# Softmax factors inside the turning matrix, the compressed rows as one block, and the scan's sample rows for all channel blocks at once

## The chip, the cores and the metric

The kernel runs on one core of one Trainium2 chip. The metric is device time in microseconds, the median of several executions. Engines are named as in the profile: PE (TensorE matmul), PEld (its weight load), DVE (VectorE), ACT (ScalarE), POOL (GpSimd) and SP (SyncE, which here only issues DMAs).

## What is computed

One inference step of two trunk layers over 520 rows: a prompt of 512 positions and 8 sample rows of one position each, model width 1024. Layer 0 is a Mamba-2 scan (2048 channels in 16 blocks of 128) beside an attention branch of 16 heads of 64, joined by one output projection; layer 1 is a convolution module; behind each stands a ConvFFN. The parts that the change touches, shortened:

```python
# attention, per query row t and head h: two softmaxes that are used here
p_c = masked_softmax(s_c, m_c)         # over 31 compressed rows
p_s = masked_softmax(s_s, m_s)         # selected rows (for the prompt: all earlier rows)
p_w = masked_softmax(s_w, m_w)         # window rows
o = g[..., 0:1] * (p_c @ vc) + g[..., 1:2] * (p_s @ vs) + g[..., 2:3] * (p_w @ vw)

# scan, a sample row: one step of the recurrence from a stored state
h_t = exp(dt * a) * h_0 + dt * outer(x, B);  y = C @ h_t + d_skip * x
y = rms_norm((y * silu(z)) per group)
out = concat([y_ssm, y_nsa]) @ w_out
```

All tensors are fp32, and the products of the large weights are kept to fp32 quality by splitting.

## The kernel before

**Split products.** A weight or an activation is split into hi + lo (`split`, L292 to L294: ACT copies to hi, DVE subtracts to lo), and a product is three matmuls (`mm3`, L312 to L314). `wload` (L296) stages a weight block of 128x1024 in a buffer of the pool `raw` (three buffers, open for the whole kernel), from where `split` writes it to a second pool.

**Attention.** `attention(hg)` runs for four groups of four heads, each over four blocks `b` of 128 query rows: 16 steps. A step forms scores of 128x`nw` for `nw = 128*(b+1)` keys, selected (`r=0`) and window (`r=1`) apart, and exponentials `pt` (`Ps`). It multiplies each `pt` by gate over sum (`mx[:, 2]`), 8 scalings a step, some on ACT (L1178), the others on DVE (L1180). Then `turned` (L1182) turns four blocks of 128x128 by PE transposes against the identity into `pT`, splits it into `pth` and `ptl`, and two matmuls of 512 columns add V times these to `po` (L1199, L1200). A step has 2(b+1) such parts and one last part for the compressed rows `pc`, where `pT` has 32 partitions. Between the steps, up to 32 blocks of another projection, `xz_tile` (48 matmuls each), and steps of the sample rows' attention are issued; they fill PE while softmax work goes on elsewhere. The last three steps have little of this left.

**Scan.** `scan_group(g, beside)` runs for four groups of four channel blocks t. Each of the 16 steps loads rows `xs` and `cum`, builds decays and does chunk products; seven small DVE operations (L1387 to L1395) of 8 columns serve its sample rows. `beside` issues blocks of the output projection (kg=0) between. After the scan `begin` (L1652) opens the residual `h` and the pools of the next layers, and the kg=1 third of the output projection follows from `wout` (L1283). `state_rows` finishes the sample states on DVE, two pieces a step.

**What sets the order.** A scheduler with a simulated timeline orders the instructions of each engine and frees pool buffers by dependence; pool sizes and the side on which a pool lies decide which loads can be issued early.

Of the kernel before, what the change touches and what calls it, by code (L numbers as in the profile page):

```python
# [40 lines left out]
ACT_NORM = (0, 2)  # L41
# [217 lines left out]
def step_kernel(ctx: ExitStack, tc: tile.TileContext, I, O):  # L259
# [4 lines left out]
    P["raw"] = ctx.enter_context(tc.tile_pool(name="raw", bufs=3, side="right"))  # L264
# [12 lines left out]
    def VV(name):  # L277
        o, n = VEC[name]
        return vec[:, o:o + n]
# [404 lines left out]
    def mixer(begin):  # L684
# [43 lines left out]
        VC = ap.tile([32, 2, 2, 64], F32R, name="VC")  # L728
# [23 lines left out]
        b2v = tp.tile([64, 128], F32, name="b2v", bufs=1)  # L752
# [5 lines left out]
        def behind_x(hf, ins):  # L758

            with tc.issue_after(ins):  # L760
# [6 lines left out]
                nc.scalar.dma_start(b2v, I["b2v"].to_broadcast([64, 128]))  # L767
# [112 lines left out]
        for kv in range(2):  # L880
# [44 lines left out]
        def compress(b):  # L925
# [4 lines left out]
            for kv in range(2):  # L930
# [20 lines left out]
                else:  # L951
                    for g in range(2):
                        nc.tensor.matmul(ps[0:64, g * 64:g * 64 + 64], hid[:, g], w2[:, 128:192], start=True, stop=True)
                    nc.vector.scalar_tensor_tensor(vcS[:, b], ps[0:64], 0.5, b2v, op0=ALU.mult, op1=ALU.add)
# [39 lines left out]
        def xz_tile(g, t):  # L994
# [20 lines left out]
            nc.sync.dma_start(spill[g * 10 + t], th)  # L1015

# [85 lines left out]
        def attention(hg, rows_of):  # L1102
            g = hg // 2
            qh = tp.tile([128, 2, S], F32, tag="qh", name="qh", bufs=1)
            nc.sync.dma_start(qh, d_q[hg])
            for b in range(4):
                step = 4 * hg + b
                nw = 128 * (b + 1)
                QS = tp.tile([128, 4, 128], F32R, tag="QS", name="QS")
                for par in range(2):  # L1110
                    sl, ot = slice(par * 64, par * 64 + 64), slice(64 - par * 64, 128 - par * 64)
                    src = qh[sl, :, b * 128:b * 128 + 128]
# [20 lines left out]
                pc = tp.tile([128, 4, 32], F32, tag="pc", name="pc", bufs=2)  # L1133
# [40 lines left out]
                for hh in range(4):  # L1174
                    for r in range(2):
                        p = Ps[hh][:, r, 0:nw]
                        if r == 0 and b in ACT_NORM:
                            nc.scalar.activation(p, p, AF.Copy, scale=mx[:, 2, hh, r:r + 1])  # L1178
                        else:
                            nc.vector.tensor_scalar(p, p, mx[:, 2, hh, r:r + 1], None, op0=ALU.mult)  # L1180

                def turned(ps4, kn):  # L1182

                    pT = gen(512, "pT")
                    for hh in range(4):
# [116 lines left out]
        def scan_group(g, beside):  # L1302
# [21 lines left out]
            if g >= HG:  # L1324
                later = state_rows(tp, g)
# [372 lines left out]
```

## Time and profile before

| what | value |
|---|---|
| runs shown | 1958.25, 1958.77 and 1962.19 us, median 1958.77 |
| profiled execution | 1961.67 us, of which its span is 1959.9 |
| PE busy | 94% of the span, clock 0.97 on average |
| DVE, ACT, POOL busy | 72%, 50%, 10% |
| attention, 280 to 668 us; scan, 668 to 860 us | 388 and 192 us |

The table's first line is the time of executions with no profile beside it; the profiled one is 2.9 us above their median. A matmul row's duration includes its way through the pipeline, so the distance from one start to the next says more of PE's demand than the duration does. The stretches are cut where the profile's rows change: from 280 to 610 the attention's steps have projection blocks between them, from 610 to 668 they have nearly none, and 856.8 to 874.2 is the border between the scan and the rest.

### The profile page before, as it was taken

What the parts mean: (1) busy time and instruction counts of PE and PEld (TensorE: products, weight loads), DVE (VectorE), ACT (ScalarE), POOL (GpSimd) and SP (SyncE); (2) the same over time, 40 slices, a digit from 0 to 9 for tenths busy, and PEclk for the clock granted to TensorE, in tenths of its full rate; (3) what the DMA queues carried; (4) which work ended last, traced back from release to release, by engine and by line L of the source; (5) the groups of instructions that cost most, each with busy time, mean ns of one, the idle gap of its engine ahead of it and who ended that gap; (6) DMA issues with size and microseconds to landing.
All of it is one profiled execution on the core that took longest, in us unless ns stands there. A gap on an engine that the chain in (4) does not pass through costs nothing.

```text
span 1959.9 us, 38005 instructions
## 1 busy us (share of the span) xinstructions
PE 1835.2 (94%) x14449; PEld 1706.1 (87%) x14449; DVE 1415.3 (72%) x3385; ACT 974.4 (50%) x2093; POOL 189.5 (10%) x226
## 2 busy tenths in 40 slices
PE   6998889999998799998999999999989899999997
PEld 5997888988887588987999999998667789999997
DVE  5764768888887698968667766574786865666766
ACT  3223446676666577646555433355127755444433
POOL 0000021101000003130000211001111000000000
PEclk9999998999998799989999999999999999999999
DMA  8446254444321274543245433222433223444421
GB/s 296 114 140 197 76 190 130 149 138 129 126 90 57 92 243 136 157 143 100 87 143 165 132 105 109 87 81 53 119 107 119 87 87 116 122 119 120 148 62 49
DMA packets 125947, 240.90 MB, mean 123 GB/s; under 512 B 16499, under 2 KB 63236, under 8 KB 125444
## 3 DMA queue, kind: packets, MB, share of 16 engines
q1 hardware_dynamic: 120676, 221.45, 36.9%
q0 software_dynamic: 4000, 13.73, 2.2%
q10 hardware_dynamic: 1088, 3.29, 0.5%
q8 instruction: 114, 1.87, 0.4%
q14 instruction: 69, 0.57, 0.1%
HBM read 200.75 MB, written 30.88 MB: 118 GB/s over the span
## 4 chain that ended last, share of the span: by engine, by line
PE 43%; DVE 5%; ACT 3%; DMA 2%; issue 1%; SPq 0%; POOL 0%; DVEq 0%; ACTq 0%; POOLq 0%
PE up L312 8%; PE up L313 8%; PE up L314 8%; PE dn L312 4%; PE dn L313 4%; PE dn L314 4%; PE dn L624 2%; PE pw L312 1%; PE pw L313 1%; PE pw L314 1%; PE ns L333 1%; DMA raw_dn<-in_w_down 1%; DVE xf L385 1%; DVE h L387 1%; DVE facc L631 1%
## 5 line engine op out<-in xcount | busy, mean ns | idle before, releaser
L312 PE MATMUL dn<-gh,wh_dn 128*128 128x256 f32 (+1 forms) x704 | 198.0, 285 | 4.8 <-ACT gh L463 2.6
L314 PE MATMUL dn<-gh,wl_dn 128*128 128x256 f32 (+1 forms) x704 | 198.9, 284 | 0.0
L313 PE MATMUL dn<-gl,wh_dn 128*128 128x256 f32 (+1 forms) x704 | 198.4, 283 | 0.0
L451 DVE SCALAR_TENSOR_TENSOR c<-up,vec,c 128x511 f32<-128x511 f32 (+2 forms) x216 | 138.9, 645 | 16.1 <-ACT c L448 15.7
L312 PEld LDWEIGHTS dn<-gh,wh_dn 128*128 128x128 f32 x704 | 131.5, 189 | 6.8 <-DVE facc L478 3.7
L313 PEld LDWEIGHTS dn<-gl,wh_dn 128*128 128x128 f32 x704 | 133.1, 189 | 0.1
L314 PEld LDWEIGHTS dn<-gh,wl_dn 128*128 128x128 f32 x704 | 132.8, 189 | 0.0
L464 POOL TENSOR_TENSOR gl<-gm,gh 128x520 fp32r<-128x520 f32 (+2 forms) x54 | 61.8, 1145 | 700.6 <-ACT gh L463 700.5
L446 DVE TENSOR_TENSOR up<-up,rsx 128x520 f32<-128x520 f32 (+2 forms) x108 | 65.0, 603 | 81.5 <-PE up L314 79.9
L478 DVE TENSOR_TENSOR facc<-dn,facc 128x256 f32<-128x256 f32 (+1 forms) x160 | 66.2, 423 | 66.4 <-PE dn L314 66.1
L293 ACT ACTIVATE wh_up<-raw_up 128x1024 fp32r<-128x1024 f32 x68 | 72.0, 1058 | 71.8 <-PE up L313 46.5
L312 PE MATMUL acc<-x0hm,wh_xz 128*128 128x256 f32 x320 | 96.3, 301 | 6.9 <-ACT u L1001 4.5
L294 DVE TENSOR_TENSOR wl_up<-raw_up,wh_up 128x1024 fp32r<-128x1024 f32 x68 | 83.1, 1222 | 23.0 <-ACT wh_up L293 22.9
L314 PE MATMUL acc<-x0hm,wl_xz 128*128 128x256 f32 x320 | 94.3, 295 | 0.0
L313 PE MATMUL acc<-x0lm,wh_xz 128*128 128x256 f32 x320 | 94.1, 294 | 0.0
L313 PE MATMUL acc<-x1lm,wh_xz 128*128 128x264 f32 x320 | 92.8, 290 | 0.0
L312 PE MATMUL acc<-x1hm,wh_xz 128*128 128x264 f32 x320 | 92.6, 289 | 0.0
L448 ACT ACTIVATE c<-up,vec 128x520 f32<-128x520 f32 (+2 forms) x108 | 74.9, 695 | 34.8 <-DVE up L446 34.4
L314 PE MATMUL acc<-x1hm,wl_xz 128*128 128x264 f32 x320 | 92.1, 288 | 0.0
L293 ACT ACTIVATE wh_dn<-raw_dn 128x1024 fp32r<-128x1024 f32 (+1 forms) x48 | 47.4, 988 | 87.7 <-PE dn L313 62.8
L294 DVE TENSOR_TENSOR ptl<-pT,pth 128x512 fp32r<-128x512 f32 (+1 forms) x96 | 65.0, 684 | 25.8 <-ACT pth L293 25.6
L293 ACT ACTIVATE pth<-pT 128x512 fp32r<-128x512 f32 (+1 forms) x96 | 56.3, 595 | 53.1 <-PE pT L1186 49.9
(584 smaller groups left out, 6859.7 us busy)
## 6 DMA issues: line engine op xcount, KB each, us to landing
raw_up<-in_w_up SPq DMA_DIRECT2D x68, 512.0 KB, 3.8
raw_xz<-in_w_in SPq DMA_DIRECT2D x40, 512.0 KB, 4.8
raw_dn<-in_w_down SPq DMA_DIRECT2D x32, 512.0 KB, 3.7
raw_wo<-in_w_out SPq DMA_DIRECT2D x24, 512.0 KB, 4.2
raw_pw<-in_w_pw SPq DMA_DIRECT2D x24, 512.0 KB, 3.8
spill<-uth SPq DMA_DIRECT2D x40, 260.0 KB, 2.0
st<-in_st SPq DMA_DIRECT2D x40, 256.0 KB, 4.2
cc<-in_c_cmp SPq DMA_DIRECT2D x64, 128.0 KB, 2.6
```

The source lines that it names most:

```text
L293: nc.scalar.activation(hi, src, AF.Copy)
L294: (eng or nc.vector).tensor_sub(lo, src, hi.bitcast(F32))
L312: nc.tensor.matmul(ps, hi[:, wc], xh, start=first, stop=False)
L313: nc.tensor.matmul(ps, hi[:, wc], xl, start=False, stop=False)
L314: nc.tensor.matmul(ps, lo[:, wc], xh, start=False, stop=last)
L333: nc.tensor.matmul(ps, ones, acc[:, :n], start=i < group, stop=i == len(ks) - 1)
L446: nc.vector.tensor_mul(u(a, e0), u(a, e0), rv[:, a:e0])
L448: nc.scalar.activation(c[:, rs], u(r0, r1), AF.Identity, bias=V("fb", l * 44 + mt), scale=W(2, mt))
L451: nc.vector.scalar_tensor_tensor(c[:, a:e], u(a - d, e - d), W(2 - d, mt), c[:, a:e], op0=ALU.mult, op1=ALU.add)
L464: nc.gpsimd.tensor_sub(gl[:, rs], gm[:, rs], gh[:, rs].bitcast(F32))
L478: nc.vector.tensor_add(f, ps, f)
L624: nc.tensor.matmul(ps[i * 32:i * 32 + 32], cw[m][:, 4 * q + i], x4[m][:, i, cs], start=q == 0, stop=q == NQ[m] - 1)
```

## The change

Four edits and what they need of memory. (1) The factors `mx[:, 2]` are no longer applied to `pt`: one DVE product makes a tile `dg` of eight diagonal blocks (identity times factor), and each 128x128 block of `pt` is turned by an ordinary fp32 matmul against its diagonal block. (2) The compressed rows of four heads are turned as one 128x128 block, with `VC` padded to a block diagonal, and stand first in `po`. (3) `qh` is loaded per step. (4) The sample rows of the scan: their first part is computed once for all 16 channel blocks (`sample_rows`), the rest once a group (`sample_group`), `cum` of these rows comes by two DMAs of their own, and `state_rows` for the last group start with group 2. The pool `raw` becomes two: `rawm` with two buffers until the scan's end, and a new `raw` with three that `begin` opens.

```diff
-    P["raw"] = ctx.enter_context(tc.tile_pool(name="raw", bufs=3, side="right"))
...
-        VC = ap.tile([32, 2, 2, 64], F32R, name="VC")
+        VC = ap.tile([128, 2, 4, 2, 64], F32R, name="VC")
...
+                hid4 = tp.tile([128, 2, 4, 32], F32, tag="cc4", name="chid4", bufs=1)
+                nc.vector.tensor_copy(hid4, hid[:, :, None, :].to_broadcast([128, 2, 4, 32]))
-                    nc.tensor.matmul(ps[0:32, g * 64:g * 64 + 64], hid[:, g], w2[:, 128:192], start=True, stop=True)
-                vc = tp.tile([32, 2, 64], F32, tag="ub", name="vcP", bufs=2)
-                nc.vector.scalar_tensor_tensor(vc.rearrange("p g d -> p (g d)"), ps[0:32], 0.5, b2v[0:32], op0=ALU.mult,
-                                               op1=ALU.add)
-                split(VC[:, :, 0], VC[:, :, 1], vc)
+                    nc.tensor.matmul(ps[:, g * 64:g * 64 + 64], hid4[:, g].rearrange("p h c -> p (h c)"), w2[:, 128:192],
+                                     start=True, stop=True)
+                vc = tp.tile([128, 2, 64], F32, tag="ub", name="vcP", bufs=2)
+                nc.vector.scalar_tensor_tensor(vc.rearrange("p g d -> p (g d)"), ps, 0.5, b2v, op0=ALU.mult, op1=ALU.add)
+                nc.vector.memset(VC.bitcast(F32), 0.0)
+                for hh in range(4):
+                    rw = slice(32 * hh, 32 * hh + 32)
+                    split(VC[rw, :, hh, 0], VC[rw, :, hh, 1], vc[rw])
...
+            if t < 4:
+                nc.gpsimd.tensor_copy(smp[:, m, 0], th[:, S:T])
...
-            qh = tp.tile([128, 2, S], F32, tag="qh", name="qh", bufs=1)
-            nc.sync.dma_start(qh, d_q[hg])
+                qh = tp.tile([128, 2, 128], F32, tag="qh", name="qh", bufs=2)
+                nc.sync.dma_start(qh, d_q[hg][:, :, b * 128:b * 128 + 128])
-                    src = qh[sl, :, b * 128:b * 128 + 128]
+                    src = qh[sl]
...
-                pc = tp.tile([128, 4, 32], F32, tag="pc", name="pc", bufs=2)
+                pc = tp.tile([128, 4, 32], F32, tag="pc", name="pc", bufs=1)
...
+
+                dg = tp.tile([128, 4, 2, 128], F32, tag="dg", name="dg", bufs=1)
+                nc.vector.tensor_mul(dg.rearrange("p h r q -> p (h r) q"), ident[:, None, :].to_broadcast([128, 8, 128]),
+                                     mx[:, 2].rearrange("p h r -> p (h r)")[:, :, None].to_broadcast([128, 8, 128]))
+
+                def parted(pT):
+                    ph, pl = (tp.tile([128, 512], F32R, tag="pt" + p, name="pt" + p, bufs=THB)[:, :pT.shape[-1]]
+                              for p in "hl")
+                    split(ph, pl, pT)
+                    return ph, pl
+
+
+                po = gen(512, "po")
+
+                pT = gen(128, "pT")
+                nc.tensor.transpose(pT, pc.rearrange("p h k -> p (h k)"), ident)
+                ph, pl = parted(pT)
+                    for p in (ph, pl):
+                        nc.tensor.matmul(po[:, hh * 128:hh * 128 + 128], VC[:, g, hh].rearrange("p a d -> p (a d)"), p,
+                                         start=hh == 0 and p is ph, stop=False)
+                for n in range(b + 1):
-                        p = Ps[hh][:, r, 0:nw]
-                        if r == 0 and b in ACT_NORM:
-                            nc.scalar.activation(p, p, AF.Copy, scale=mx[:, 2, hh, r:r + 1])
-                        else:
-                            nc.vector.tensor_scalar(p, p, mx[:, 2, hh, r:r + 1], None, op0=ALU.mult)
-
-                def turned(ps4, kn):
-
-                    pT = gen(512, "pT")
-                    for hh in range(4):
-                        nc.tensor.transpose(pT[0:kn, hh * 128:hh * 128 + 128], ps4[hh], ident)
-                    ph, pl = (tp.tile([128, 512], F32R, tag="pt" + p, name="pt" + p, bufs=THB)[0:kn] for p in "hl")
-                    split(ph, pl, pT[0:kn])
-                    return ph, pl
-
-
-                po = gen(512, "po")
-                parts = [(VB[:, 1 - r, n, g], [p[:, r, n * 128:n * 128 + 128] for p in Ps], 128)
-                         for n in range(b + 1) for r in range(2)]
-                parts.append((VC[:, g], [pc[:, hh] for hh in range(4)], 32))
-                for k, (v, ps4, kn) in enumerate(parts):
-                    ph, pl = turned(ps4, kn)
-                    v = v.rearrange("p a d -> p (a d)")
-                    nc.tensor.matmul(po, v, ph, start=k == 0, stop=False)
-                    last = nc.tensor.matmul(po, v, pl, start=False, stop=k == len(parts) - 1)
+                        pT = gen(512, "pT")
+                        for hh in range(4):
+                            nc.tensor.matmul(pT[:, hh * 128:hh * 128 + 128], Ps[hh][:, r, n * 128:n * 128 + 128],
+                                             dg[:, hh, r], start=True, stop=True)
+                        ph, pl = parted(pT)
+                        v = VB[:, 1 - r, n, g].rearrange("p a d -> p (a d)")
+                        nc.tensor.matmul(po, v, ph, start=False, stop=False)
+                        last = nc.tensor.matmul(po, v, pl, start=False, stop=n == b and r == 1)
...
-            cum = pool.tile([128, 2, 528], F32, tag="cum", name="cum", bufs=1 if g == t == 0 else XSB)
+            cum = pool.tile([128, 2, S], F32, tag="cum", name="cum", bufs=1 if g == t == 0 else XSB)
-            q.dma_start(cum, d_rows[k:k + 2, :].rearrange("(o h) t -> o h t", o=1).to_broadcast([128, 2, 528]))
+            q.dma_start(cum, d_rows[k:k + 2, 0:S].rearrange("(o h) t -> o h t", o=1).to_broadcast([128, 2, S]))
...
+
+
+        cd = tp.tile([128, 16, 2 * NB], F32, name="cumS")
+        for r in range(2):
+            nc.gpsimd.dma_start(cd[r * 64:r * 64 + 64], d_rows[r::2, S:528].rearrange("(o m) t -> o m t", o=1)
+                                .to_broadcast([64, 16, 2 * NB]))
+        xsk = tp.tile([128, 16, NB], F32, name="xskS")
+
+        def sample_rows():
+
+            nc.scalar.activation(smp[:, :, 1], cd[:, :, 0:NB], AF.Exp)
+            nc.vector.tensor_mul(xsk, smp[:, :, 0], VV("dsk")[:, :, None].to_broadcast([128, 16, NB]))
+            nc.vector.tensor_mul(smp[:, :, 0], smp[:, :, 0], cd[:, :, NB:])
+
+        def sample_group(g, y, bcs):
+
+            gs = slice(4 * g, 4 * g + 4)
+            ys = tp.tile([128, 4, NB], F32, tag="ys", name="ys", bufs=2)
+            nc.vector.tensor_mul(hC[:, gs], hC[:, gs], smp[:, gs, 1])
+            nc.vector.tensor_mul(ys, smp[:, gs, 0], bcs[:, 1][:, None, :].to_broadcast([128, 4, NB]))
+            nc.vector.tensor_add(hC[:, gs], hC[:, gs], xsk[:, gs])
+            nc.vector.tensor_add(y[:, :, S:T], hC[:, gs], ys)
...
-            if g >= HG:
-                later = state_rows(tp, g)
+            if g == HG - 1:
+                later = state_rows(tp, HG)
+            if g == 0:
+                sample_rows()
-                E = tp.tile([128, T], F32, tag="E", name="E", bufs=EB)
+                E = tp.tile([128, S], F32, tag="E", name="E", bufs=EB)
-                    nc.scalar.activation(E[sl, 128:T], cum[sl, r, 128:T], AF.Exp)
+                    nc.scalar.activation(E[sl, 128:S], cum[sl, r, 128:S], AF.Exp)
...
-
-                dtx, es = smp[:, 4 * g + t, 0], E[:, S:T]
-                nc.vector.tensor_copy(smp[:, 4 * g + t, 1], es)
-                ys = tp.tile([128, 2, NB], F32, tag="ys", name="ys", bufs=2)
-                for r in range(2):
-                    sl = slice(r * 64, r * 64 + 64)
-                    nc.vector.tensor_mul(dtx[sl], xs[sl, S:T], cum[sl, r, T:528])
-                nc.vector.tensor_mul(ys[:, 0], hC[:, 4 * g + t], es)
-                nc.vector.tensor_mul(ys[:, 1], dtx, bcs[:, 1])
-                nc.vector.tensor_add(ys[:, 0], ys[:, 0], ys[:, 1])
-                nc.vector.scalar_tensor_tensor(y[:, t, S:T], xs[:, S:T], V("dsk", 4 * g + t), ys[:, 0],
-                                               op0=ALU.mult, op1=ALU.add)
+                if t == 0:
+                    sample_group(g, y, bcs)
...
+        P["raw"] = ctx.enter_context(tc.tile_pool(name="raw", bufs=3))
-    with tc.tile_pool(name="wum", bufs=3, side="right") as P["wu"]:
+    with tc.tile_pool(name="rawm", bufs=2, side="right") as P["raw"], \
+            tc.tile_pool(name="wum", bufs=3, side="right") as P["wu"]:```

The last attention step on PE. Names: `pT` is the turned block, `pth` and `ptl` its halves, `VB` and `VC` the values, `cst` the identity, `dg` the diagonal blocks. Before:

```order
L1186 MATMUL pT<-cst_77,pt 128x128 x4
L1199 MATMUL po<-pth,VB 128x512
L1200 MATMUL po<-ptl,VB 128x512
L1186 MATMUL pT<-cst_77,pc 32x128 x4
L1199 MATMUL po<-pth,VB 128x512
L1200 MATMUL po<-ptl,VB 128x512
L1639 MATMUL oT<-cst_77,osS 128x128
L1199 MATMUL po<-pth,VC 128x512
L1200 MATMUL po<-ptl,VC 128x512
```

The same step after the change:

```order
L1198 MATMUL po<-pth,VC 128x128
L1198 MATMUL po<-ptl,VC 128x128
L1204 MATMUL pT<-dg,pt 128x128 x8
L1208 MATMUL po<-pth,VB 128x512
L1209 MATMUL po<-ptl,VB 128x512
L1204 MATMUL pT<-dg,pt 128x128 x4
L1208 MATMUL po<-pth,VB 128x512
L1209 MATMUL po<-ptl,VB 128x512
```

The compressed part has moved from the end of the step to its beginning, and each turn is now a matmul against `dg`.

The border after the scan on SP, the DMA issues up to the first weights of the next layers. Names: `raw_wo` stages w_out, `raw_us` the next layer's w_up, `hst`, `Bb`, `st` belong to states. Before:

```order
L302 DMA raw_wo<-in_w_out 128x1024
L1331 DMA zt<-spill_151 128x520
L1358 DMA o_sp<-hst 128x128
L302 DMA raw_wo<-in_w_out 128x1024
L1358 DMA o_sp<-hst 128x128
L1467 DMA Bb<-d_bc 128x4x128
L1472 DMA st<-in_st 128x512
L302 DMA raw_wo<-in_w_out 128x1024
L1472 DMA st<-in_st 128x512
L1658 DMA h<-in_x 128x8x256
L1658 DMA h<-in_x 128x8x264
L302 DMA raw_wo<-in_w_out 128x1024 x3
```

The same border after the change:

```order
L1391 DMA o_sp<-hst 128x128
L1364 DMA zt<-spill_151 128x520
L1391 DMA o_sp<-hst 128x128 x3
L1490 DMA Bb<-d_bc 128x4x128
L1495 DMA st<-in_st 128x512 x2
L1681 DMA h<-in_x 128x8x256
L1681 DMA h<-in_x 128x8x264
L300 DMA raw_wo<-in_w_out 128x1024 x8
L300 DMA raw_us<-in_w_up 128x1024 x6
```

All eight loads of the kg=1 weights now stand behind the load of `h`; before, five of them stood ahead of it (three are in these rows, two in earlier ones).

## Rows read from the trace of the kernel before

**Rows 1.** The page: busy time of each engine, and the chain of waits by engine

```profile
PE 1835.2 (94%) x14449; PEld 1706.1 (87%) x14449; DVE 1415.3 (72%) x3385; ACT 974.4 (50%) x2093; POOL 189.5 (10%) x226
...
PE 43%; DVE 5%; ACT 3%; DMA 2%; issue 1%; SPq 0%; POOL 0%; DVEq 0%; ACTq 0%; POOLq 0%
```

**Rows 2.** Four stretches: length, busy us (instructions) of each engine, clock, DMA share, GB/s

```profile
280.00:610.00 330.00, 317.51 (x2460) 288.36 (x2460) 279.65 (x921) 213.50 (x537) 29.22 (x44) 0.97 0.41 128
340.00:360.00 20.00, 20.00 (x174) 18.24 (x174) 18.59 (x49) 14.12 (x32) 1.59 (x3) 1.00 0.39 115
610.00:668.00 58.00, 47.98 (x190) 31.78 (x191) 41.21 (x116) 31.28 (x78) 0.00 (x0) 0.76 0.07 21
668.00:860.00 192.00, 176.13 (x1409) 160.62 (x1409) 171.24 (x501) 132.66 (x338) 41.44 (x44) 0.95 0.54 170
```

**Rows 3.** Groups on PE, 280 to 610 | busy us, mean ns

```profile
L1186 PE MATMUL pT<-cst,pt 128*128 128x128 f32 x248 | 40.9, 273 | 0.0
L1186 PE MATMUL pT<-cst,pc 128*32 128x128 f32 x52 | 7.8, 272 | 0.0
```

**Rows 4.** Timeline of PE, four turns: start, us from first to last end

```profile
582.02 0.60 PE L1186 MATMUL pT<-cst,pt 128*128 128x128 f32 x4
```

**Rows 5.** Timeline of PE, four matmuls of F32 operands in the scan

```profile
723.90 1.06 PE L1349 MATMUL states<-xde,BT 128*128 128x128 f32 x8
724.79 0.60 PE L1341 MATMUL xT<-cst,xs 128*128 128x128 f32 x4
```

**Rows 6.** Timeline of PE, a product of the compressed rows

```profile
568.77 0.49 PE L1199 MATMUL po<-pth,VC 32*128 32x512 f32 x1
569.19 0.38 PE L313 MATMUL acc<-x0lm,wh_xz 128*128 128x256 f32 x1
```

**Rows 7.** Groups on DVE, 280 to 670 | busy us, mean ns | idle before

```profile
L1180 DVE TENSOR_SCALAR pt<-pt,mx 128x256 f32<-128x256 f32 (+3 forms) x96 | 31.1, 389 | 0.2
L294 DVE TENSOR_TENSOR wl_xz<-raw_xz,wh_xz 128x1024 fp32r<-128x1024 f32 x29 | 35.3, 1218 | 5.3 <-ACT wh_xz L293 5.3
L294 DVE TENSOR_TENSOR ptl<-pT,pth 128x512 fp32r<-128x512 f32 (+1 forms) x96 | 65.0, 684 | 25.8 <-ACT pth L293 25.6
L1141 DVE TENSOR_TENSOR pc<-pc,mc 128x128 f32<-128x128 f32 x16 | 4.5, 283 | 0.1
```

**Rows 8.** Groups on ACT, the same stretch

```profile
L1178 ACT ACTIVATE pt<-pt,mx 128x128 f32<-128x128 f32 (+1 forms) x32 | 13.6, 503 | 1.3 <-DVE mx L1173 1.3
L293 ACT ACTIVATE pth<-pT 128x512 fp32r<-128x512 f32 (+1 forms) x96 | 56.3, 595 | 53.1 <-PE pT L1186 49.9 <-DVE ptl L294 2.2 <-DVE mx L1128 0.5
```

**Rows 9.** Waits, 280 to 670: who, for whom; us in total, times, longest

```profile
ACT wh_xz L293 <- PE acc L313: 11.6, 11, 2.7
```

**Rows 10.** Timeline, last attention step

```profile
648.19 0.20 DVE L1172 RECIPROCAL mx<-mx 128x8 f32<-128x8 f32 x1 [0.31 <-ACT pt L1169]
652.99 0.60 ACT L293 ACTIVATE pth<-pT 128x512 fp32r<-128x512 f32 x1 [3.94 <-PE pT L1186]
```

**Rows 11.** Timeline at the border after the scan

```profile
856.80 0.58 PE L312 MATMUL acc<-x0hs,wh_wo 128*128 128x256 f32 x1 [0.22 <-ACT x0hs L293]
863.39 1.35 SPq L1658 DMA_DIRECT2D h<-in_x  x2
863.39 2.96 ACT L293 ACTIVATE wh_wo<-raw_wo 128x1024 fp32r<-128x1024 f32 x3 [1.51 <-POOL x1ls L294]
865.74 3.43 SPq L302 DMA_DIRECT2D raw_wo<-in_w_out  x3
```

**Rows 12.** Busy time by stretch, the border

```profile
856.80:874.20 17.40, 16.63 (x105) 15.31 (x106) 9.93 (x14) 6.42 (x13) 6.47 (x8) 0.80 0.54 191
```

**Rows 13.** Chain of waits at the border: start, us, what

```profile
865.74 8.29 DMA raw_wo<-in_w_out
```

**Rows 14.** Groups on DVE in the scan, two of the six removed

```profile
L1391 DVE TENSOR_TENSOR smp<-xs,cum 64x8 f32<-64x8 f32 x30 | 5.5, 184 | 4.7 <-DMA cum<-d_rows 2.6 <-DMA xs<-spill 1.8
L1392 DVE TENSOR_TENSOR ys<-hC,E 128x8 f32<-128x8 f32 x16 | 2.5, 157 | 0.0
```

More of the change, by code (lines that the diff above doesn't have):

```diff
@@ L40 @@
 HOLD = 6
-ACT_NORM = (0, 2)
 NQ = (5, 4, 4, 4, 4, 6, 7, 7)
@@ L751, in mixer @@
         w2 = tp.tile([128, 192], F32, name="w2", bufs=1)
-        b2v = tp.tile([64, 128], F32, name="b2v", bufs=1)
+        b2v = tp.tile([128, 128], F32, name="b2v", bufs=1)
         pe = tp.tile([128, 2, 2, 8], F32, name="pe", bufs=1)
@@ L766, in behind_x @@
                 nc.scalar.dma_start(alr, I["alr"].to_broadcast([128, 32]))
-                nc.scalar.dma_start(b2v, I["b2v"].to_broadcast([64, 128]))
+                nc.scalar.dma_start(b2v, I["b2v"].to_broadcast([128, 128]))
                 nc.scalar.dma_start(pe.rearrange("p a b c -> p (a b c)"), I["pe"])
@@ L953, in compress @@
                         nc.tensor.matmul(ps[0:64, g * 64:g * 64 + 64], hid[:, g], w2[:, 128:192], start=True, stop=True)
-                    nc.vector.scalar_tensor_tensor(vcS[:, b], ps[0:64], 0.5, b2v, op0=ALU.mult, op1=ALU.add)
+                    nc.vector.scalar_tensor_tensor(vcS[:, b], ps[0:64], 0.5, b2v[0:64], op0=ALU.mult, op1=ALU.add)
         prep, scores_of, softmaxes = nsa_sample(mp, gen, C, tp, knew, qs, kcS, PT, pnT, gS, gather)
@@ L1173, in attention @@
                 nc.vector.tensor_mul(mx[:, 2], mx[:, 2], gTsw[:, b, 4 * hg:4 * hg + 4])
-                for hh in range(4):
-                    for r in range(2):
-                        p = Ps[hh][:, r, 0:nw]
-                        if r == 0 and b in ACT_NORM:
-                            nc.scalar.activation(p, p, AF.Copy, scale=mx[:, 2, hh, r:r + 1])
-                        else:
-                            nc.vector.tensor_scalar(p, p, mx[:, 2, hh, r:r + 1], None, op0=ALU.mult)
-                def turned(ps4, kn):
-                    pT = gen(512, "pT")
-                    for hh in range(4):
-                        nc.tensor.transpose(pT[0:kn, hh * 128:hh * 128 + 128], ps4[hh], ident)
-                    ph, pl = (tp.tile([128, 512], F32R, tag="pt" + p, name="pt" + p, bufs=THB)[0:kn] for p in "hl")
-                    split(ph, pl, pT[0:kn])
+                dg = tp.tile([128, 4, 2, 128], F32, tag="dg", name="dg", bufs=1)
@@ new lines, in attention @@
+                nc.tensor.transpose(pT, pc.rearrange("p h k -> p (h k)"), ident)
[7 more added lines that the diff above has]
+                        pT = gen(512, "pT")
+                        for hh in range(4):
+                            nc.tensor.matmul(pT[:, hh * 128:hh * 128 + 128], Ps[hh][:, r, n * 128:n * 128 + 128],
[4 more added lines that the diff above has]
+                        last = nc.tensor.matmul(po, v, pl, start=False, stop=n == b and r == 1)
@@ L1300, in nsa_out @@
             return part
+        cd = tp.tile([128, 16, 2 * NB], F32, name="cumS")
+        for r in range(2):
+            nc.gpsimd.dma_start(cd[r * 64:r * 64 + 64], d_rows[r::2, S:528].rearrange("(o m) t -> o m t", o=1)
[12 more added lines that the diff above has]
+            nc.vector.tensor_add(y[:, :, S:T], hC[:, gs], ys)
         def scan_group(g, beside):
@@ L1385, in scan_group @@
                     next(later, None)
-                dtx, es = smp[:, 4 * g + t, 0], E[:, S:T]
-                nc.vector.tensor_copy(smp[:, 4 * g + t, 1], es)
-                ys = tp.tile([128, 2, NB], F32, tag="ys", name="ys", bufs=2)
-                for r in range(2):
-                    sl = slice(r * 64, r * 64 + 64)
-                    nc.vector.tensor_mul(dtx[sl], xs[sl, S:T], cum[sl, r, T:528])
-                nc.vector.tensor_mul(ys[:, 0], hC[:, 4 * g + t], es)
-                nc.vector.tensor_mul(ys[:, 1], dtx, bcs[:, 1])
-                nc.vector.tensor_add(ys[:, 0], ys[:, 0], ys[:, 1])
-                nc.vector.scalar_tensor_tensor(y[:, t, S:T], xs[:, S:T], V("dsk", 4 * g + t), ys[:, 0],
-                                               op0=ALU.mult, op1=ALU.add)
+                if t == 0:
+                    sample_group(g, y, bcs)
                 nc.vector.tensor_mul(y[:, t], y[:, t], zt)
@@ L1664, in begin @@
         return after
-    with tc.tile_pool(name="wum", bufs=3, side="right") as P["wu"]:
+    with tc.tile_pool(name="rawm", bufs=2, side="right") as P["raw"], \
+            tc.tile_pool(name="wum", bufs=3, side="right") as P["wu"]:
         new = mixer(begin)()
```

## The prediction, made before the result was known

> **What bounds the kernel now.** I read the page first: PE is busy for 94% of the span, DVE for 72%, and the chain that ended last goes through PE for 43% and through DVE for 5% [rows 1]. PE is therefore the engine to count on, but an average over the whole span says nothing of the parts that change, so the second view is the busy time by stretch [rows 2]. The attention with projection blocks between its steps (280 to 610 us) has PE busy for 317.5 of 330 us and DVE for 279.7; its last steps (610 to 668) have PE for 48.0 of 58 at a granted clock of 0.76; the scan (668 to 860) has PE for 176.1 and DVE for 171.2 of 192.
>
> Busy time overstates PE, because the rows of pipelined matmuls overlap. Its real demand I take from a stretch in which it never rests: 340 to 360, with 174 matmuls in 20.0 us at full clock [rows 2], which is 0.115 us each. The 2460 matmuls of 280 to 610 then ask for 283 us, 86% of the stretch, which leaves 47 us of slack in pieces; the 1409 of the scan ask for 162 of 192. PE is nearly the bound in the attention, and DVE (85% busy there) is close behind. The third view is the list of waits and groups: ACT's conversion `pth` stands idle for 49.9 us because PE has not yet turned `pT` [rows 8]. The engine that is waited for in the attention is PE, and its turns are what is waited for.
>
> **The turns.** A transpose on PE is one record; four of them last 0.60 us, with 0.27 for one, so they follow each other every (0.60-0.27)/3 = 0.11 us [rows 3, 4]. An ordinary matmul of two fp32 operands with 128 columns is seen in the scan: four matmuls have eight records, and the next work starts 0.89 us after the first [rows 5], 0.22 each. The change makes all 320 turns of `pt` (16 steps, 20 blocks on average) into such matmuls, so each costs 0.11 more: 35.8 us of PE in all, 27.8 for the 248 that stand before 610 [rows 3] and 8.1 for the 72 behind.
>
> That this is the wrong direction is also a rule: the Trainium skill's page "Perfetto Trace Analysis", section "Transposes", says to make a logical transpose by the transpose instruction and not by a standard matmul, since it skips the arithmetic. The trace agrees, with 0.11 against 0.22 us.
>
> **The compressed rows.** Turning them as one block takes three of four turns away, 39 of 52 before 610 [rows 3]: -4.3 us. Their product has 32 partitions and 512 columns and takes 0.42 us [rows 6], 0.84 a step; eight of 128 columns take 0.92 at 0.115 each. That is +0.08 a step, +1.0 before 610. PE's demand there rises by 27.8-4.3+1.0 = 24.5 us.
>
> **What DVE and ACT lose.** The 96 scalings on DVE go, 31.1 us; 16 products for `dg` come, each of 128x1024 as the weights' subtraction is, 1.22 us [rows 7], 19.5 us. The compressed part's `ptl` shrinks from about 0.68 to the 0.28 of an operation of 128x128 [rows 7], 16 times: -6.4. DVE's net is -18. ACT loses 13.6 us of scalings [rows 8].
>
> **280 to 610.** PE gets 24.5 us more to do in 330 us with 47 us of slack, and DVE and ACT get 14 to 18 less. If every slack could be filled the time would not change, or would fall a little where a turn had waited for a scaling; if none, it grows by 24.5. The stretch has full parts (340 to 360) and emptier ones, so I take the middle, +12, and keep 0 to +24.
>
> **610 to 668.** The 72 turns cost 8.1 us at full clock and 10.7 at 0.76; 12 compressed turns go, -1.7. But the scalings stand in series here: in the last step the reciprocal starts at 648.19 and the first `pth` at 652.99 [rows 10], 4.8 us. With `dg` the same way is two small operations (0.4), one of 1.2 and four turns of 0.22 at half clock (1.8): 3.4. Three steps save about 4 us, and the compressed part is no longer the last, about 2. Sum +3, bounds -2 and +9.
>
> **The border after the scan.** This is the pool's price and not the turns'. Before, five of the eight weight blocks of the kg=1 product had been issued ahead of `h`; PE starts on them at 856.80 [rows 11] and does 105 matmuls until 874.2 [rows 12], 12.6 us of work at 0.12 each, while the next loads, issued at 865.74 behind `h`, take 8.29 us [rows 13]. After, the new `raw` is opened after `h`, and all eight loads stand behind it in SP's queue: the load of `h` cannot begin before 863.4 (where its issue stands now, [rows 11]), two issues take 1.35, one load 8.29, one conversion about 1.0: PE's first kg=1 matmul comes at about 874, and the 12.6 us of work start there. With some of it at the lower clock after the pause (the stretch now shows 0.80 with far less rest, [rows 12]) I take +14. If a single load takes only some 4 us, as one finds an empty queue, 70 matmuls are late instead of 105: +8; with four more at low clock, +18.
>
> **The scan.** Six lines of small operations go, 22 us of DVE with L1391 the dearest (5.5) and L1392 the cheapest (2.5) [rows 14]; 18 operations on more columns come, about 4. DVE falls by 18 of 171. But PE has 84% to do, and the first steps wait for their loads (L1391 itself waited for `cum` and `xs`, [rows 14]), which stay. I take -3, from -12 (DVE gives back most) to +3 (the new sample rows stand ahead of the first step).
>
> **The rest.** `rawm` has two buffers instead of three. The split `wh_xz` waits 11.6 us for PE and for no load [rows 9], so the third buffer was not what fed it: 0, at worst +5. The 16 `qh` loads of a quarter each, the POOL copies and the two loads of `cum` for the sample rows (many short runs) lie beside the attention. +1, from -2 to +5.
>
> **Sum.** 12+3+14-3+1 = +27. On the profiled execution (1961.67, of which 1.8 lie around the span) that is 1988.7; that execution stands 2.9 above the median of the runs, so on the median 1985.8, say 1986.
>
> **Rivals.** *DVE was the bound.* DVE is 85% busy in the attention and 89% in the scan, and PE's extra may fit in its 47 us of slack. Then the relief shows: -15 in the attention, -12 in the scan, +14 at the border, 1946. It decides if PE's slack lies next to the turns. Against it speak the 49.9 us that `pth` waits for PE. Chance 0.14.
>
> *The border stays.* If PE finds other work, or the loads come early after all, the 14 us are not paid: 1972. The order speaks against it: nothing of kg=1 stands ahead of `h`. Chance 0.15.
>
> *Two staging buffers are too few.* If each of the 29 projection blocks of this stretch [rows 7] were late by a microsecond, it costs 29 more: 2015. It decides when a load takes longer than a block, and a block has over 10 us (330 over 29). Chance 0.08.
>
> *An fp32 turn costs twice what the scan shows.* If a turn against `dg` took four records' time, it would add 3x0.11 instead of 0.11: 72 us more PE demand, of which the filled stretch hides none; 1986+72 = 2058. Rows 5 show two records and 0.22. Chance 0.02. The Trainium skill's page "FP8 and Floating Point Precision", section "TensorE Precision Notes", gives a true fp32 product four passes; by that the time would be this rival's if each pass cost as much as a transpose, and the trace shows half of it.
>
> *Gains and losses cancel.* Full use of slack, a small border: within 3.9 us of 1958.8. Chance 0.08.
>
> **How the numbers follow.** The forecast has 0.53, with a range of its own of 1966 to 2006 (the terms' bounds, not all at one end). To hold 8 in 10 with the border case and part of the cancelling one, the range is 1958 to 2008. A difference of 0.2%, 3.9 us, is about what a measurement of this kernel can tell from none. Faster has 0.14, the same 0.08; slower 0.78, which is the forecast, the border case and the two dear ones.
>
> **What would show it.** Right: `pT` has 640 matmul records at 0.11 distance; DVE's busy time before 668 falls by about 18; 280 to 668 is 10 to 20 us longer; PE rests for over 10 us between the scan's end and the first `raw_wo` landing. Wrong: an attention that is shorter (then DVE was the bound), kg=1 matmuls ahead of the load of `h`, waits of `wh_xz` for `raw_xz`, or a scan shorter by more than 10 us.

## The result and the profile after

The changed kernel takes 1988.49 us (median; 1985.11 to 1990.87) against 1958.51 of the kernel before in the same comparison: 1.0144 times as long, interval 1.0127 to 1.0161. The forecast was 1986, its range 1958 to 2008. The profiled execution took 1989.85 us, its span is 1988.1, 28.2 longer than before's 1959.9.

The page after, its line of busy times and its line of the chain by engine, beside [rows 1]:

```profile
PE 1849.0 (93%) x14817; PEld 1745.8 (88%) x14817; DVE 1395.1 (70%) x3216; ACT 961.6 (48%) x2067; POOL 192.8 (10%) x244
...
PE 69%; DVE 11%; DMA 8%; ACT 5%; issue 4%; SPq 2%; POOL 1%; DVEq 0%; ACTq 0%; POOLq 0%
```

PE is busy for 13.8 us more in a span 28.2 us longer, and DVE for 20 less. So half of the loss is work, the other half is rest, and the chain now goes through DMA for 8% of the span where it had 2%. The stretches show where; those of before [rows 2] were cut at fixed times, these at the kernel's own marks (first query conversion, last projection block, last product of the attention, load of `h`), and the last two are the border:

```profile
266.90:629.00 362.10, 350.36 (x2860) 333.77 (x2859) 280.45 (x890) 210.23 (x538) 31.55 (x60) 0.99 0.41 127
629.00:671.50 42.50, 38.46 (x231) 31.96 (x229) 28.26 (x68) 22.28 (x54) 0.00 (x0) 0.92 0.09 26
671.50:863.30 191.80, 169.76 (x1386) 155.42 (x1386) 163.14 (x412) 130.75 (x340) 49.19 (x50) 0.97 0.52 158
855.30:874.70 19.40, 0.00 (x0) 0.00 (x0) 6.22 (x9) 5.08 (x11) 7.91 (x10) 0.55 0.54 182
874.80:881.00 6.20, 6.18 (x27) 5.87 (x28) 3.97 (x4) 3.17 (x3) 0.00 (x0) 0.50 0.64 215
```

And the same two stretches of the attention of the kernel before:

```profile
269.60:609.50 339.90, 326.24 (x2530) 296.62 (x2528) 283.61 (x928) 217.06 (x544) 30.75 (x46) 0.97 0.42 133
609.50:665.80 56.30, 46.09 (x179) 30.38 (x179) 40.67 (x113) 31.18 (x79) 0.00 (x0) 0.76 0.07 22
```

To read them: the attention is 396.2 us long before and 404.6 after. PE's busy time in it rises from 372.3 to 388.8, and its rest falls from 23.9 to 15.8. DVE's busy time falls from 324.3 to 308.7. In the border PE does nothing at all from 855.3 to 874.7, where before it did 105 matmuls [rows 12], and it comes back at clock 0.50.

The turns, as the tile's rows have them (compare [rows 3]), then the last step's diagonal blocks and one part of it (compare [rows 10]):

```profile
L1204 PE MATMUL pT<-dg,pt x640: 270/275/582, 299.7 to 669.8; 128*128 128x128 f32 x160
L1194 PE MATMUL pT<-cst,pc x16: 270/328/330, 286.9 to 651.2; 128*128 128x128 f32 x16
```

```profile
655.95 1.22 DVE L1181 TENSOR_TENSOR dg<-cst,mx 128x1024 f32<-128x1024 f32 x1
663.41 1.05 PE L1204 MATMUL pT<-dg,pt 128*128 128x128 f32 x8
664.22 0.48 PE L1208 MATMUL po<-pth,VB 128*128 128x512 f32 x1
```

All 320 turns have two records each. The eight records of a part start every (1.05-0.275)/7 = 0.11 us and the product behind them 0.81 us after the first, about 0.2 for a turn against 0.11 before. Behind the diagonal blocks' product (1.22 us) no scaling stands any more. Groups on DVE, then on ACT, 280 to 675 us, as in [rows 7, 8]:

```profile
L1181 DVE TENSOR_TENSOR dg<-cst,mx 128x1024 f32<-128x1024 f32 x16 | 19.5, 1220 | 0.5
L292 DVE TENSOR_TENSOR ptl<-pT,pth 128x512 fp32r<-128x512 f32 (+1 forms) x96 | 59.0, 618 | 37.0 <-ACT pth L291 36.7
```

```profile
L291 ACT ACTIVATE pth<-pT 128x512 fp32r<-128x512 f32 (+1 forms) x96 | 51.5, 546 | 53.2 <-PE pT L1204 50.3 <-DVE ptl L292 2.3 <-PE pT L1194 0.2
```

The diagonal blocks cost what the weights' subtraction costs, 16 x 1.22. `pth` still stands idle for PE's turns for 50.3 us, as before (49.9).

The border, beside [rows 11]: SP's issues, the first conversion, the first kg=1 matmul.

```profile
863.28 1.33 SPq L1681 DMA_DIRECT2D h<-in_x  x2
864.66 19.61 SPq L300 DMA_DIRECT2D raw_wo<-in_w_out  x8
873.66 1.06 ACT L291 ACTIVATE wh_wo<-raw_wo 128x1024 fp32r<-128x1024 f32 x1 [11.22 <-DMA raw_wo<-in_w_out]
874.77 0.58 PE L310 MATMUL acc<-x0hs,wh_wo 128*128 128x256 f32 x1 [19.51 <-ACT wh_wo L291]
```

All the kg=1 loads stand behind `h`; the first matmul is at 874.77, after 19.51 us without one.

### The profile page after: what moved, and what is told of

Its sections match the earlier page's. It is cut to its first block, busy times and chain, and to the rows that moved or that the text cites. A ratio compares the mean times of both kernels' runs of the same rounds, so it can differ in the third digit from the quotient of the medians.

```text
span 1988.1 us, 38622 instructions
## 1 busy us (share of the span) xinstructions
PE 1849.0 (93%) x14817; PEld 1745.8 (88%) x14817; DVE 1395.1 (70%) x3216; ACT 961.6 (48%) x2067; POOL 192.8 (10%) x244
## 4 chain that ended last, share of the span: by engine, by line
PE 69%; DVE 11%; DMA 8%; ACT 5%; issue 4%; SPq 2%; POOL 1%; DVEq 0%; ACTq 0%; POOLq 0%
PE up L310 8%; PE up L311 8%; PE up L312 8%; PE acc L310 5%; PE acc L311 5%; PE acc L312 5%; PE dn L310 5%; PE dn L311 4%; PE dn L312 4%; PE pT L1204 3%; PE cmpAB L939 2%; PE dn L622 2%; PE pw L310 1%; PE pw L311 1%; PE pw L312 1%
## 5 line engine op out<-in xcount | busy, mean ns | idle before, releaser
L310 PE MATMUL dn<-gh,wh_dn 128*128 128x256 f32 (+1 forms) x704 | 197.9, 285 | 3.9 <-ACT gh L461 2.6
L312 PE MATMUL dn<-gh,wl_dn 128*128 128x256 f32 (+1 forms) x704 | 199.2, 284 | 0.0
L311 PE MATMUL dn<-gl,wh_dn 128*128 128x256 f32 (+1 forms) x704 | 198.7, 283 | 0.0
L310 PEld LDWEIGHTS dn<-gh,wh_dn 128*128 128x128 f32 x704 | 131.9, 189 | 5.1 <-ACT gh L461 2.9
L311 PEld LDWEIGHTS dn<-gl,wh_dn 128*128 128x128 f32 x704 | 133.5, 190 | 0.1
L312 PEld LDWEIGHTS dn<-gh,wl_dn 128*128 128x128 f32 x704 | 133.1, 189 | 0.0
L291 ACT ACTIVATE wh_up<-raw_up 128x1024 fp32r<-128x1024 f32 x68 | 72.0, 1059 | 72.9 <-PE up L311 49.1
L310 PE MATMUL acc<-x0hm,wh_xz 128*128 128x256 f32 x320 | 94.2, 294 | 5.7 <-ACT u L1004 2.9
L292 DVE TENSOR_TENSOR wl_up<-raw_up,wh_up 128x1024 fp32r<-128x1024 f32 x68 | 83.0, 1221 | 22.5 <-ACT wh_up L291 22.3
L312 PE MATMUL acc<-x0hm,wl_xz 128*128 128x256 f32 x320 | 93.1, 291 | 0.0
L311 PE MATMUL acc<-x0lm,wh_xz 128*128 128x256 f32 x320 | 92.5, 289 | 0.0
L310 PE MATMUL acc<-x1hm,wh_xz 128*128 128x264 f32 x320 | 92.4, 289 | 0.0
L311 PE MATMUL acc<-x1lm,wh_xz 128*128 128x264 f32 x320 | 92.4, 289 | 0.0
L312 PE MATMUL acc<-x1hm,wl_xz 128*128 128x264 f32 x320 | 92.1, 288 | 0.0
L291 ACT ACTIVATE wh_dn<-raw_dn 128x1024 fp32r<-128x1024 f32 (+1 forms) x48 | 47.5, 989 | 88.3 <-PE dn L311 63.4
L1204 PEld LDWEIGHTS pT<-dg,pt 128*128 128x128 f32 x640 | 83.3, 196 | 6.0 <-DVE dg L1181 2.6
L1204 PE MATMUL pT<-dg,pt 128*128 128x128 f32 x640 | 85.9, 280 | 2.3 <-DVE dg L1181 2.3
```

What stands on the lines that cost most here:

```text
L291: nc.scalar.activation(hi, src, AF.Copy)
L292: (eng or nc.vector).tensor_sub(lo, src, hi.bitcast(F32))
L310: nc.tensor.matmul(ps, hi[:, wc], xh, start=first, stop=False)
L311: nc.tensor.matmul(ps, hi[:, wc], xl, start=False, stop=False)
L312: nc.tensor.matmul(ps, lo[:, wc], xh, start=False, stop=last)
L1204: nc.tensor.matmul(pT[:, hh * 128:hh * 128 + 128], Ps[hh][:, r, n * 128:n * 128 + 128], dg[:, hh, r], start=True, stop=True)
```

## The experiments

The table has every kernel's median and the lengths of its stretches in the profiled execution (us): attention from the first query conversion to the last product `po`; scan from there to the issue of the load of `h`; border from there to the last kg=1 matmul of two hi halves; the rest to the end. The time ahead of the attention, 266 to 276 us, has no column. The code of the rest differs in nothing but the staging pool, and yet it lies between 1049 and 1061 in all but e2, with either pool; so a difference of some 6 us in one stretch of one profiled execution is not evidence by itself. Nor is the profiled execution always near its kernel's median: e3's is 6.9 us above it, e4's 5.1 below.

| run | median | attention | scan | border | rest |
|---|---|---|---|---|---|
| before | 1959.9 | 396.2 | 197.6 | 43.6 | 1052.9 |
| changed | 1988.5 | 404.6 | 191.8 | 63.6 | 1061.2 |
| e1 pools alone | 1985.1 | 397.5 | 194.8 | 66.6 | 1056.8 |
| e2 changed, one pool of two | 1995.8 | 405.0 | 197.1 | 46.2 | 1078.7 |
| e3 changed, transposes | 1962.5 | 378.2 | 193.8 | 69.3 | 1057.7 |
| e4 sample rows alone | 1959.8 | 394.1 | 194.1 | 43.1 | 1054.7 |
| e5 block and query loads | 1947.8 | 380.5 | 194.8 | 43.8 | 1060.4 |
| e6 pools and diagonal blocks | 2000.7 | 411.4 | 194.7 | 64.9 | 1052.4 |
| e7 pools and block | 1963.8 | 380.8 | 195.7 | 66.5 | 1049.2 |
| e8 query loads alone | 1953.8 | 394.4 | 192.5 | 42.3 | 1053.3 |
| e9 changed, one-record turns | 1970.1 | 377.9 | 200.3 | 65.7 | 1054.2 |
| e10 pools and block, last | 1992.1 | 406.3 | 192.5 | 63.7 | 1060.4 |
| e11 pools and narrow turns, first | 1988.5 | 393.1 | 195.5 | 62.8 | 1058.5 |
| e12 all but turns and pools | 1937.6 | 376.1 | 195.1 | 41.7 | 1052.8 |

The median of before moved between 1959.9 and 1961.1 in the three comparisons (e1 to e4, e5 to e8, e9 to e12); ratios are to the one of the same comparison, with 95% intervals. Where a run of one comparison is set against a run of another, as e6, e7, e10 and e11 are against e1, that microsecond comes on top of the noise.

**e1, the pools alone.**

```diff
-    P["raw"] = ctx.enter_context(tc.tile_pool(name="raw", bufs=3, side="right"))
...
+        P["raw"] = ctx.enter_context(tc.tile_pool(name="raw", bufs=3))
...
+    with tc.tile_pool(name="rawm", bufs=2, side="right") as P["raw"], \
...
```

> The kernel before with the change of the staging pool alone (two buffers until the scan's end, a new pool with three behind the load of h). Theory, the pool is the border's price: PE rests for 15 to 20 us between the scan and the first kg=1 matmul and the time rises by 14 to 20 us, to 1973 to 1979; the attention stays as long as it was. Rival A, the border's gap comes from the new order of the scan and not from the pool: within 4 us of 1958.5. Rival B, two buffers also feed the attention too late: the attention grows by over 5 us, and the time passes 1983.

1985.07, ratio 1.0132 (1.0118 to 1.0147). The load of `h` and the first kg=1 matmul on the timeline:

```profile
861.50 1.35 SPq L1657 DMA_DIRECT2D h<-in_x  x2
872.87 0.58 PE L311 MATMUL acc<-x0hs,wh_wo 128*128 128x256 f32 x1 [17.90 <-ACT wh_wo L292]
```

PE rests 17.9 us there with nothing else changed. The attention is 1.3 us longer than before (397.5). Its weights' conversion `wh_xz` now waits for a load once, 3.5 us, which it never did before; that is all that shows of the two buffers there. The border is 23 us longer and the scan 3 shorter (46 kg=1 matmuls that had been done before the load of `h` now stand behind it): 20 net, and the whole is 25 slower, more than was expected. Where the other 5 lie these rows don't tell.

**e2, one pool of two buffers.** The changed kernel with `raw` opened once, `bufs=2`, on the right, and neither of the two new pools.

> The changed kernel with one staging pool of two buffers open for the whole kernel, in place of the two pools. Theory: kg=1 loads can be issued ahead of the load of h again, two instead of three; the gap at the border shrinks from 19.5 to under 10 us, and the time falls by 8 to 16 us, to 1972 to 1980. Rival: two buffers are too few for the later layers, whose weights come in turn with the work: the border's gain is given back there, 1985 or more. If the border's gap is not the pool's, the gap stays near 19 us.

1995.77, ratio 1.0186 (1.0171 to 1.0200). The border is back to 46.2, so the gap there is the late opening. But the rest grows by 17.5, and the median is 7 above the changed kernel's. The waits of the next layers, `wh_up` for its loads, in the changed kernel and here:

```profile
ACT wh_up L291 <- DMA raw_up<-in_w_up: 23.3, 9, 7.1
```

```profile
ACT wh_up L292 <- DMA raw_up<-in_w_up: 39.1, 18, 5.5
```

The rival held as well: with two buffers in the later layers ACT waits 39.1 us for `raw_up` in place of 23.3. Two buffers are enough in the mixer and too few behind it.

**e3, transposes again.** The scalings stand again where `dg` was made; shown here are the turns alone.

```diff
-                            nc.tensor.matmul(pT[...], Ps[hh][...], dg[:, hh, r], start=True, stop=True)
+                            nc.tensor.transpose(pT[...], Ps[hh][...], ident)
```

> The changed kernel with the 320 turns as transposes again and the scalings on DVE and ACT as before, no diagonal blocks; the compressed rows, the sample rows, the query loads and the pools stay as changed. Theory, PE is the bound of the attention and an ordinary fp32 turn costs 0.11 us more: the attention gets 8 to 14 us shorter, the time is 1975 to 1981. Rival, DVE is the bound: the 18 us of scalings come back and the time is 1990 or more.

1962.51, ratio 1.0015 (1.0005 to 1.0026): 26 us less than the changed kernel, twice what was expected, and the attention shows it (404.6 to 378.2). DVE is not the bound. What was not foreseen is that the attention falls 18 us below that of before.

**e4, the sample rows alone.** The edits (4) of the change on the kernel before.

> The kernel before with the treatment of the scan's sample rows alone (once for all channel blocks, their own loads, states of the last group begun a group earlier). Theory, DVE bounds the scan beside PE: the scan is 5 to 9 us shorter and the time 1950 to 1954. Rival, PE and loads bound it: within 4 us of 1958.5.

1959.77, ratio 1.0005 (0.9993 to 1.0016). The scan of the profiled execution is 3.5 us shorter, the median shows nothing: the rival.

**e5, block and query loads without the pools.** As the diff of the change, with `VC` unchanged and one group's block diagonal built from it:

```diff
+            if hg % 2 == 0:
+                vx[0] = tp.tile([128, 4, 2, 64], F32R, tag="VX", name="VX", bufs=1)
+                nc.vector.memset(vx[0].bitcast(F32), 0.0)
+                for hh in range(4):
+                    nc.scalar.activation(vx[0][32 * hh:32 * hh + 32, hh], VC[:, g].bitcast(F32), AF.Copy)
```

> The kernel before with the compressed rows as one block ahead of the other parts and the query loads per step; transposes, scalings, sample rows and the staging pool as before. (The block-diagonal values of one of the two key groups stand in a tile that eight small ACT copies fill, since the memory has no room for both.) Theory, these two edits shorten the attention by 18 us (378 in place of 396 us, as the run with transposes showed beside the pools) and the pool's price of 25 us is not paid: 1938 to 1946. Rival, the 18 us were the new pools' order and not these edits: 1955 to 1962.

1947.78, ratio 0.9931 (0.9907 to 0.9954; its six runs lie between 1940 and 1954), just above the theory's span: the attention is 380.5 and the border 43.8, as the theory has it; a rest of 1060.4 took part of it in the profiled execution.

**e6, diagonal blocks on the pools alone.** `dg` and the turns as in the change, the compressed part as before.

> The kernel before with the new staging pools and the diagonal blocks alone (the compressed rows last and in 32 columns, as before), to stand against the run with the pools alone, 1985. Theory, every extra microsecond of PE counts because the attention is full: 26 to 36 us more, 2011 to 2021. The blind sum's term for this edit, 12 to 15 us: 1997 to 2000. Rival, the dear turn is only dear together with the other edits: under 1995.

2000.69, ratio 1.0211 (1.0193 to 1.0230): 15.6 over e1, near the prediction's term and below the theory. The attention's two stretches in e1, then e6, then e3:

```profile
269.20:610.80 341.60, 326.57 (x2516) 296.07 (x2516) 284.46 (x928) 216.85 (x543) 32.83 (x46) 0.97 0.42 131
610.80:666.70 55.90, 44.78 (x179) 29.70 (x178) 39.57 (x110) 31.39 (x78) 0.00 (x0) 0.82 0.07 22
```

```profile
272.20:640.80 368.60, 356.19 (x2820) 331.78 (x2821) 286.99 (x895) 216.65 (x539) 29.71 (x46) 0.98 0.39 122
640.80:683.60 42.80, 38.04 (x197) 29.77 (x196) 26.92 (x62) 21.73 (x52) 0.00 (x0) 0.84 0.08 25
```

```profile
268.60:599.80 331.20, 322.38 (x2598) 299.95 (x2596) 282.89 (x938) 218.20 (x558) 28.98 (x60) 0.99 0.45 138
599.80:646.80 47.00, 39.27 (x170) 27.00 (x170) 35.25 (x101) 26.45 (x66) 0.00 (x0) 0.82 0.09 26
```

From e1 to e6 PE's busy time rises by 22.8 us (371.4 to 394.2) and its rest falls by 8.9 (26.1 to 17.2), so 14 reach the attention. From e3 to the changed kernel the busy time rises by 27.1 and the rest by less than one down (16.5 to 15.8): 26 reach it. The block edit had already used up rest that could hide part of the dear turns: with it alone on the pools (e7, next) PE rests 17.8 us. That this is why the same turns cost more is argued from these rows and not tested by itself, since e3 differs from e1 by the query loads and the sample rows too.

**e7, the block on the pools alone.** As the change's second edit, with `parted` and the narrow products, transposes kept.

> The kernel before with the new staging pools and the compressed rows as one block, first in the product; query loads per group of heads, as before. To stand against the pools alone, 1985. Theory A, the block edit carries the gain of the attention (a part that needs no softmax of the long rows is ready early, and fewer turns): 1965 to 1970. Theory B, the query loads carry it: 1980 to 1986.

1963.82, ratio 1.0016 (1.0002 to 1.0029): 21 under e1, theory A. The attention is 17 us shorter, half of it busy time of PE (371.4 to 363.0), half rest (26.1 to 17.8). Its two stretches in e7 (those of e1 stand above), then the waits of `pth` for the turns, e1 and e7:

```profile
266.30:599.10 332.80, 322.08 (x2587) 300.49 (x2585) 282.83 (x940) 217.78 (x559) 25.47 (x46) 0.98 0.44 136
599.10:647.10 48.00, 40.89 (x171) 28.26 (x171) 35.25 (x101) 26.40 (x65) 0.00 (x0) 0.79 0.08 25
```

```profile
ACT pth L292 <- PE pT L1185: 59.3, 43, 3.9
```

```profile
ACT pth L292 <- PE pT L1206: 42.6, 31, 4.0
```

**e8, query loads alone.**

```diff
-            qh = tp.tile([128, 2, S], F32, tag="qh", name="qh", bufs=1)
+                qh = tp.tile([128, 2, 128], F32, tag="qh", name="qh", bufs=2)
```

> The kernel before with the query loads per step alone. Theory A, the block edit carries the gain: within 4 us of 1959.9. Theory B, the loads carry it, since a step's first operation waits for a load of 512 KB at each new group of heads: 1941 to 1950.

1953.82, ratio 0.9967 (0.9955 to 0.9979): 7 us gained, between the two theories. The attention shows 2 of them, no more than noise.

**e9, one-record turns.**

```diff
-                    pt = tp.tile([128, 2, 512], F32, tag="pt", name="pt", bufs=5)
+                    pt = tp.tile([128, 2, 512], F32R, tag="pt", name="pt", bufs=5)
-                dg = tp.tile([128, 4, 2, 128], F32, tag="dg", name="dg", bufs=1)
+                dg = tp.tile([128, 4, 2, 128], F32R, tag="dg", name="dg", bufs=1)
```

> The changed kernel whose exponentials and diagonal blocks are stored rounded to fp32r, so that the 320 turns are one-record matmuls of 0.11 to 0.12 us (their low halves are left out of the product; all else as changed). Theory, the second record of each turn is the 26 us: the attention falls from 405 to 370 to 382 us and the time to 1953 to 1968. Rival, the diagonal block in series (one DVE product of 1.22 us before the first turn) or its buffer is the price: the attention stays above 395 and the time above 1978.

1970.08, ratio 1.0046 (1.0028 to 1.0064), 18 under the changed kernel and 2 above the expected span. The turns in this kernel, and its attention:

```profile
L1204 PE MATMUL pT<-dg,pt x320: 218/274/476, 298.4 to 642.5; 128*128 128x128 f32 x160
```

```profile
266.70:607.30 340.60, 327.12 (x2620) 306.96 (x2619) 280.55 (x896) 210.86 (x539) 28.47 (x60) 0.98 0.43 135
607.30:644.60 37.30, 32.14 (x149) 23.81 (x147) 26.37 (x64) 21.21 (x52) 0.00 (x0) 0.86 0.09 29
```

Half the records, and the attention is 377.9, e3's length, with the diagonal blocks' product still in it. So in the attention the second record of each turn is the whole 26 us, and the product in series costs nothing that shows. Of the time, 18 of the 26 come back: the total is 7.6 above e3. The profiled scan is 6.5 longer, for which no run here gives a cause. The kernel is not one to put in the change's place, as its turns drop the low halves.

**e10 and e11, place and form of the compressed part.** In e10 the lines of the block's part stand behind the loop over `n`; in e11:

```diff
-                parts.append((VC[:, g], [pc[:, hh] for hh in range(4)], 32))
+                parts.insert(0, (VC[:, g], [pc[:, hh] for hh in range(4)], 32))
```

> The kernel before with the new staging pools and the compressed rows as one block, but as the last part of the product, as they stood before. To stand against the pools alone (1985) and the block first (1964). Theory A, standing first is what saves the time: 1978 to 1986. Theory B, the block itself is (three of four turns fewer, shorter splits): 1962 to 1970.

> The kernel before with the new staging pools and the compressed rows in four narrow turns as before, but as the first part of the product. Theory A, standing first saves the time: 1964 to 1972. Theory B, the block saves it: 1980 to 1986.

1992.09 (1.0157, 1.0135 to 1.0179) and 1988.45 (1.0142, 1.0121 to 1.0163). Neither theory held alone: the block put last is 7 us above e1, the narrow turns put first 3 above it (its attention is 4 shorter but began 6.8 later). Both intervals overlap e1's, so that either costs time is not shown; that neither gains is. Only block and first place together give the 21. Each of these kernels has its last projection block at another place (592.0 in e10, 599.1 in e7, 610.8 in e1, 624.9 in e11), so the scheduler answers each with another interleaving. Which part of the 21 is the form and which is that interleaving stays open.

**e12, the cheap parts.** e5 with the sample rows.

> The changed kernel's cheap parts on the kernel before: block first, query loads per step, sample rows at once; transposes, scalings and staging pool as before. Theory, the sample rows free DVE in the scan once the attention is shorter: 1941 to 1946. Rival, they bring nothing here either: 1944 to 1951, as the run without them.

1937.60, ratio 0.9886 (0.9863 to 0.9908): faster than both kernels, 23.5 us under before (1961.12 in the same comparison), and below the expected span. The border here, `h` and the conversion of weights that had been loaded ahead of it:

```profile
837.99 1.34 SPq L1689 DMA_DIRECT2D h<-in_x  x2
838.00 2.95 ACT L293 ACTIVATE wh_wo<-raw_wo 128x1024 fp32r<-128x1024 f32 x3 [1.52 <-POOL x1ls L294]
```

Against e5 it is 10 us less (9 by the ratios, whose intervals just touch), though the profiled scan is no shorter (195.1 and 194.8); where the sample rows give these 10, and not in e4, the runs don't show.

## Why the prediction came out right, step by step

**The sum.** 1986 was forecast and 1988.5 measured, but the terms inside it were off in both directions, and that they cancel is luck. In the profiled execution *attention and tail*, +15 together, measured +8.4, less than the 10 to 20 that were named as its sign; it is made of +26 for the turns and -18 for the block and the query loads (e3). Border and scan together are +14.2 where +11 was forecast, the rest +8.3 for +1, and the time ahead of the attention -2.7, for which no term stood. Nor do the edits add: measured one by one, against before or against the pools alone, they come to some +12 (pools 25, diagonal blocks 15.6, block -21, query loads -7, sample rows 0), and the whole to +30.

**The turns' price** of 0.11 us more each, 35.8 in all, is what the rows show, and by e9 the second record is all that the edit costs the attention. (The rule of the Trainium skill's page "Perfetto Trace Analysis", section "Transposes", to turn by the transpose instruction, is worth 26 us here, by e3 against the changed kernel. An ordinary matmul of one record, as in e9, leaves the attention as short as the transposes do.) **The half that was to be hidden** is the step that failed: with the other edits in place 26 of the 35.8 reached the time, and PE's rest, already down to 16.5 us, took up less than one. Alone (e6) the term was right, 15.6 on the median. The slack was worked out from the kernel before, not from the kernel that the other edits make. In the tail the sum also took 12 compressed turns as gone where three come back as blocks, 0.4 us.

**The compressed rows** were taken at PE's arithmetic, -4.3 and +1.0, and some 2 us for the place. The runs give 17 us of attention. The counting of matmuls could not show it: e7 has 63 matmuls more in the attention than e1, and yet PE is busy for 8.4 us less, rests for 8.3 less, and `pth` waits less.

**The border** came as described, to the time of the first kg=1 matmul (874 forecast, 874.77 measured), but at +20 in the table and not +14. The scan of before, up to the first kg=1 matmul of the border and up to the load of `h`, shows what was left out:

```profile
665.80:856.75 190.95, 175.18 (x1410) 159.82 (x1410) 169.14 (x501) 130.93 (x333) 38.32 (x40) 0.96 0.55 171
665.80:863.40 197.60, 181.42 (x1432) 164.95 (x1433) 174.00 (x507) 134.30 (x342) 44.80 (x48) 0.94 0.53 165
```

The changed scan has 1386 matmuls. So 24 kg=1 matmuls had been done even before 856.8, and stand behind `h` now: with the 105 that were counted, 129 are late, 15.5 us at 0.12 in place of 12.6. The half clock from 874.8 to 881.0 adds 3.0 (27 matmuls in 6.2 us, 3.2 at 0.12 each), where 1.4 had been taken, and the first matmul comes 0.6 after 874.2. That is 19.1 of the 20.0. The 24 matmuls, 2.9 us, are only moved out of the scan; without them the border costs 17, within that term's bounds of 8 and 18. The pools alone (e1) cost more than the bound, 20 net and 25 on the median.

**The scan** lost 6 us in the profile where -3 was forecast; 3 are those 24 matmuls, and the median of e4 shows no gain. **The rest** (+1) shows +8 in the profiled execution, within what kernels of the same later code differ by.

**The rivals.** DVE as the bound is refuted: DVE lost 15.6 us of the attention (18 forecast) and the attention grew; e3, with the scalings back, is 26 faster. The border stays: refuted by e1. Two staging buffers too few: the sign named for it, `wh_xz` waiting for `raw_xz`, is there with 1.2 us in the changed kernel and 3.5 in e1, far from the 29 that were priced; true of the later layers (e2), but there the change keeps three. Four records for an fp32 turn: there are two. Gains and losses cancel: they don't, the kernel is 1.4% slower.

## What to carry over

A scaling that is folded into a matmul moves work from the engine with rest to the one without: price it by the records of the matmul kind that it becomes, and by the rest that is left once the other edits are in, not by today's rest. A staging pool that is opened late puts every load behind what stands ahead of it in the queue; the time is read from what the next engine could have done on early loads. And a sum that comes out right may hide two terms that are wrong; only runs of single parts told here that half of the change was worth keeping.

## What the runs showed of the hardware

A matmul of two fp32 operands of 128 columns has two records at 0.11 us, one of fp32r operands one, in the same place of the program (640 and 320 records for the same turns). After 19.4 us without a matmul PE came back at a granted clock of 0.50 (1.2 GHz) and kept it for the 6.2 us to 881.0; the 27 matmuls in that time took 0.23 us each in place of 0.12.
